# A streaming batch-norm kernel: one input piece loaded over another queue, and the store of the second half in two parts

## The chip, the cores and the metric

The kernel runs on one core of a Trainium2 chip. The metric is the device time of one execution in microseconds, lower being better. The median of three runs of the kernel before is 83.81 us, between 83.76 and 83.91. The profile shows one execution on the same core, with the bytes moved by its 16 DMA engines, the instructions of its compute engines, and the DMA issues of its two issuing queues: SP (the sync engine) and ACT (the scalar engine, which also computes).

## The reference

Inference-time batch normalization followed by a ReLU, in float32, on x of shape 32 x 128 x 32 x 32 (16.78 MB in, 16.78 MB out). Each of the 128 channels has its own mean, variance, gamma and beta:

```
normalized = (x - running_mean[c]) / sqrt(running_var[c] + eps)
out        = maximum(normalized * gamma[c] + beta[c], 0)
```

The work for one element is a multiplication, an addition and a maximum: out = relu(scale[c] * x + bias[c]) with scale = gamma / sqrt(var + eps) and bias = beta - mean * scale.

## The kernel before, in words

The 4096 rows of x (batch times channel, 1024 floats or 4 KB each) are cut into two halves t = 0 and t = 1 of 8.39 MB. In one half, partition p of the on-chip memory holds the 16 neighbouring rows p*16 to p*16+15, so one half is 128 partitions by 16 rows, a run of 64 KB per partition in DRAM. Row number j within a partition fixes the channel together with p, so each j has one column of scale and bias, one value per partition.

All of x fits on the chip, and every piece has its own buffer that is never reused. `TILES` names the pieces as (t, first j, last j): in the first half rows 0-2, 2-4, 4-8 and 8-16, in the second half one tile of all 16 rows. `LOAD_CUTS` cuts the load of that last tile in two at row 8. So there are six loads, all issued by the SP queue (line 54), in this order: 1, 1, 2, 4, 4 and 4 MB, with runs of 8, 8, 16, 32, 32 and 32 KB. A load is 128 such runs, eight on each of the 16 DMA engines.

The four parameter vectors (512 bytes each) are loaded by the ACT queue (line 61) into `raw`, 8 partitions of 16 values. PE spreads them to 128 partitions with a matmul against a 0/1 matrix `rep` built on POOL (line 76), ACT takes the square root (line 84), and DVE makes `scale_t` and `bias_t` in four short instructions (lines 86 to 92).

Then comes the loop on ACT: 32 activations in place, one per (t, j), each 128 x 1024 (line 98). After the last row of a tile, ACT itself issues the store of it (line 106); `STORE_CUTS` adds a store after the very first row. So there are six stores: rows 0, 1, 2-4, 4-8 and 8-16 of the first half (0.5, 0.5, 1, 2 and 4 MB, with runs of 4, 4, 8, 16 and 32 KB), and one store of 8 MB with runs of 64 KB for the whole second half, after its sixteenth activation.

The order on ACT is the written one (the loop stands in a manual schedule), and the order on SP is that of the loads. The framework adds the semaphore waits. It has eight DMA semaphores and hands them out in turn, so a DMA that gets a semaphore which an earlier DMA had must wait for that earlier one to land: on SP, the fourth, fifth and sixth load wait for a parameter load, another parameter load and the second load; on ACT, the last store waits for the first store. The DMA traffic of SP is queue q1 in the profile, that of ACT is q10; both are served by the same 16 DMA engines.

Of the kernel before, what the change touches and what calls it, by code (L numbers as in the profile page):

```python
# [1 line left out]

# [4 lines left out]


F32 = mybir.dt.float32
ACTF = mybir.ActivationFunctionType  # L10

J = 16

TILES = ((0, 0, 2), (0, 2, 4), (0, 4, 8), (0, 8, 16), (1, 0, 16))

LOAD_CUTS = {(1, 8)}
STORE_CUTS = {(0, 1)}


@with_exitstack
def kernel(
    ctx: ExitStack,
    tc: tile.TileContext,
    x: bass.AP,
    gamma: bass.AP,
    beta: bass.AP,
    running_mean: bass.AP,
    running_var: bass.AP,  # L30
    eps: bass.AP,
    out: bass.AP,
):
    nc = tc.nc
    B, C, H, W = x.shape
    HW = H * W
    P = nc.NUM_PARTITIONS
    assert C % J == 0 and P % (C // J) == 0 and (B * C) % (P * J) == 0
    Q = C // J
    T = B * C // (P * J)  # L40

    xr = x.rearrange("b c h w -> (b c) (h w)").rearrange("(t p j) w -> t p j w", p=P, j=J)
    outr = out.rearrange("b c h w -> (b c) (h w)").rearrange("(t p j) w -> t p j w", p=P, j=J)

    data = ctx.enter_context(tc.tile_pool(name="data", bufs=1))
    params = ctx.enter_context(tc.tile_pool(name="params", bufs=1))
    psum = ctx.enter_context(tc.tile_pool(name="psum", bufs=1, space=bass.MemoryType.PSUM))

    tiles = []
    for t, a, b in TILES:  # L50
        xt = data.tile([P, b - a, HW], F32, name=f"x{t}_{a}")
        cuts = [a] + [j for j in range(a + 1, b) if (t, j) in LOAD_CUTS] + [b]
        for c, d in zip(cuts, cuts[1:]):
            nc.sync.dma_start(out=xt[:, c - a : d - a, :], in_=xr[t, :, c:d, :])  # L54
        tiles.append((t, a, b, xt))

    raw = params.tile([Q, 4, J], F32, name="raw")
    for k, src in enumerate((running_var, gamma, running_mean, beta)):  # L60
        nc.scalar.dma_start(out=raw[:, k, :], in_=src.rearrange("(q j) -> q j", j=J))
    eps_t = params.tile([P, 1], F32, name="eps_t")
    nc.vector.memset(eps_t, float(eps))  # L63
    rep = params.tile([Q, P // Q, Q], F32, name="rep")
    nc.gpsimd.memset(rep, 1.0)  # L65
    nc.gpsimd.affine_select(  # L66
        out=rep,
        in_=rep,
        compare_op=mybir.AluOpType.is_equal,
        fill=0.0,  # L70
        base=0,
        pattern=[[0, P // Q], [-1, Q]],
        channel_multiplier=1,
    )
    cols = psum.tile([P, 4, J], F32, name="cols")
    nc.tensor.matmul(  # L76
        cols.rearrange("p k j -> p (k j)"),
        rep.rearrange("q r s -> q (r s)"),
        raw.rearrange("q k j -> q (k j)"),
        start=True,  # L80
        stop=True,
    )
    std_t = params.tile([P, J], F32, name="std_t")
    nc.scalar.activation(out=std_t, in_=cols[:, 0, :], func=ACTF.Sqrt, bias=eps_t[:, 0:1], scale=1.0)  # L84
    rstd_t = params.tile([P, J], F32, name="rstd_t")
    nc.vector.reciprocal(out=rstd_t, in_=std_t)  # L86
    scale_t = params.tile([P, J], F32, name="scale_t")
    nc.vector.tensor_mul(out=scale_t, in0=cols[:, 1, :], in1=rstd_t)  # L88
    ms_t = params.tile([P, J], F32, name="ms_t")
    nc.vector.tensor_mul(out=ms_t, in0=cols[:, 2, :], in1=scale_t)  # L90
    bias_t = params.tile([P, J], F32, name="bias_t")
    nc.vector.tensor_sub(out=bias_t, in0=cols[:, 3, :], in1=ms_t)  # L92

    with tc.manual_schedule(engines={mybir.EngineType.Activation}):
        for t, a, b, xt in tiles:
            first = a
            for j in range(a, b):
                nc.scalar.activation(  # L98
                    out=xt[:, j - a, :],
                    in_=xt[:, j - a, :],  # L100
                    func=ACTF.Relu,
                    bias=bias_t[:, j : j + 1],
                    scale=scale_t[:, j : j + 1],
                )
                if j + 1 == b or (t, j + 1) in STORE_CUTS:
                    nc.scalar.dma_start(
                        out=outr[t, :, first : j + 1, :], in_=xt[:, first - a : j + 1 - a, :]
                    )
                    first = j + 1


# [1 line left out]
_INS = ['x', 'gamma', 'beta', 'running_mean', 'running_var', 'eps']  # L113
_OUTS = [((32, 128, 32, 32), 'float32')]

_NUMBERS = {'eps': 1e-05}


# [26 lines left out]
```

## Time and profile before

| what | value |
|---|---|
| median of the runs | 83.81 us (83.76 to 83.91) |
| the profiled execution's own time | 83.91 us |
| its span in the profile | 81.9 us |
| bytes read and written | 16.78 MB and 16.78 MB |
| mean rate over the span | 410 GB/s |
| ACT busy | 38.5 us, 47% of the span |
| share of 16 DMA engines taken by q1 (loads) and q10 (stores, parameters) | 48.7% and 47.7% |
| first activation of x starts | 9.49 us |
| last activation ends, its store is issued | 56.05 us, 56.08 us |

The span runs from the first to the last instruction of the profiled execution; 2.0 us of its time lie outside. The DMA rows count each DMA packet, which is one run of bytes of a transfer (4 to 64 KB here) or a completion mark of 4 bytes. A packet is booked as a whole at its start, so short windows with long packets show shares above 1 and of 0 beside each other; only their mean over several packets means anything.

### The profile page before, as it was taken

Reading aid. Unit: us, or ns where it says so; the run is one execution under the profiler, and the core shown is the slowest. Engines: PE = TensorE matmul, PEld = TensorE weight load, DVE = VectorE, ACT = ScalarE, POOL = GpSimd, SP = SyncE. Lnnn points to the kernel's source line nnn. Section 1 sums busy time; section 2 is a strip of 40 time slices with the busy share of each in tenths; the row PEclk is TensorE's granted clock in tenths of the full one; section 3 lists DMA queues with packets and bytes.
Section 4 is the critical chain, followed back from the end, with each engine's and each line's share of the span. In section 5 each row is a group of like instructions: output and inputs, shape, how many; then the busy total and the mean of one; then the engine's idle time right before and its main releaser. Section 6 shows DMA issues by size and latency. Waiting matters only on the chain.

```text
span 81.9 us, 118 instructions
## 1 busy us (share of the span) xinstructions
PE 0.7 (1%) x2; PEld 0.5 (1%) x2; DVE 0.8 (1%) x5; ACT 38.5 (47%) x34; POOL 0.8 (1%) x6
## 2 busy tenths in 40 slices
PE   0003000000000000000000000000000000000000
PEld 0002000000000000000000000000000000000000
DVE  0000300000000000000000000000000000000000
ACT  0600477799039999189995099993000000000000
POOL 3000000000000000000000000000000000000000
DMA  3799998989999997969889699997992899998290
GB/s 56 316 437 465 392 560 336 528 336 476 388 400 464 390 474 324 572 296 568 352 368 592 272 464 416 512 448 320 512 769 128 384 512 512 512 512 384 128 512 0
DMA packets 1792, 33.56 MB, mean 410 GB/s; under 512 B 256, under 2 KB 256, under 8 KB 512
## 3 DMA queue, kind: packets, MB, share of 16 engines
q1 hardware_dynamic: 864, 16.78, 48.7%
q10 hardware_dynamic: 928, 16.78, 47.7%
HBM read 16.78 MB, written 16.78 MB: 410 GB/s over the span
## 4 chain that ended last, share of the span: by engine, by line
DMA 56%; ACT 10%; issue 2%; SPq 0%
DMA x<-in_x_dram 56%; ACT x L98 10%; SPq L54 0%
## 5 line engine op out<-in xcount | busy, mean ns | idle before, releaser
L98 ACT ACTIVATE x<-x,bias_t,scale_t 128x1024 f32<-128x1024 f32 x32 | 37.0, 1227 | 10.6 <-DMA x<-in_x_dram 8.3
L84 ACT ACT_TABLE_LOAD x1 | 1.3, 1283 | 2.6 <-issue 2.6
L84 ACT ACTIVATE std_t<-cols,eps_t 128x16 f32<-128x16 f32 x1 | 0.3, 273 | 4.4 <-PE cols L76 4.4
L76 PE MATMUL cols<-raw,rep 8*128 8x64 f32 x2 | 0.7, 429 | 7.5 <-DMA raw<-in_beta_dram 7.5
L76 PEld LDWEIGHTS cols<-raw,rep 8*128 8x128 f32 x2 | 0.5, 306 | 7.5 <-issue 7.5
L66 POOL TENSOR_SCALAR_AFFINE_SELECT rep<-rep 8x128 f32<-8x128 f32 x1 | 0.4, 393 | 0.1
L86 DVE RECIPROCAL rstd_t<-std_t 128x16 f32<-128x16 f32 x1 | 0.3, 253 | 7.6 <-ACT std_t L84 7.6
L65 POOL MEMSET rep<- 8x128 f32 x1 | 0.2, 195 | 0.3 <-POOLq L126 0.3
L88 DVE TENSOR_TENSOR scale_t<-cols,rstd_t 128x16 f32<-128x16 f32 x1 | 0.2, 175 | 0.1
L92 DVE TENSOR_TENSOR bias_t<-cols,ms_t 128x16 f32<-128x16 f32 x1 | 0.2, 175 | 0.0
L90 DVE TENSOR_TENSOR ms_t<-cols,scale_t 128x16 f32<-128x16 f32 x1 | 0.2, 175 | 0.0
L126 POOL MEMSET const-bfloat16-1.0<- 128x1 bf16 x1 | 0.1, 106 | 0.0
L126 POOL MEMSET const-uint8-127<- 128x1 uint8 x1 | 0.1, 106 | 0.0
L126 POOL MEMSET const-float32-0.0<- 128x1 f32 x1 | 0.1, 103 | 0.3 <-issue 0.3
L126 POOL MEMSET const-float32-1.0<- 128x1 f32 x1 | 0.1, 103 | 0.0
L63 DVE MEMSET eps_t<- 128x1 f32 x1 | 0.1, 59 | 0.9 <-PEq L126 0.9
## 6 DMA issues: line engine op xcount, KB each, us to landing
x<-in_x_dram SPq DMA_DIRECT2D x3, 4096.0 KB, 38.7
out_dram<-x ACTq DMA_DIRECT2D x1, 4096.0 KB, 28.6
x<-in_x_dram SPq DMA_DIRECT2D x2, 1024.0 KB, 5.8
x<-in_x_dram SPq DMA_DIRECT2D x1, 2048.0 KB, 11.3
out_dram<-x ACTq DMA_DIRECT2D x1, 2048.0 KB
out_dram<-x ACTq DMA_DIRECT2D x2, 512.0 KB, 19.1
out_dram<-x ACTq DMA_DIRECT2D x1, 1024.0 KB
raw<-in_running_var_dram ACTq DMA_DIRECT2D x1, 0.5 KB
```

What stands on the lines that cost most here:

```text
L63: nc.vector.memset(eps_t, float(eps))
L65: nc.gpsimd.memset(rep, 1.0)
L66: nc.gpsimd.affine_select(out=rep, in_=rep, compare_op=mybir.AluOpType.is_equal, fill=0.0, base=0, pattern=[[0, P // Q], [-1, Q]], channel ...
L76: nc.tensor.matmul(cols.rearrange("p k j -> p (k j)"), rep.rearrange("q r s -> q (r s)"), raw.rearrange("q k j -> q (k j)"), start=True, s ...
L84: nc.scalar.activation(out=std_t, in_=cols[:, 0, :], func=ACTF.Sqrt, bias=eps_t[:, 0:1], scale=1.0)
L86: nc.vector.reciprocal(out=rstd_t, in_=std_t)
L88: nc.vector.tensor_mul(out=scale_t, in0=cols[:, 1, :], in1=rstd_t)
L90: nc.vector.tensor_mul(out=ms_t, in0=cols[:, 2, :], in1=scale_t)
L92: nc.vector.tensor_sub(out=bias_t, in0=cols[:, 3, :], in1=ms_t)
L98: nc.scalar.activation(out=xt[:, j - a, :], in_=xt[:, j - a, :], func=ACTF.Relu, bias=bias_t[:, j : j + 1], scale=scale_t[:, j : j + 1],)
L126: nc = _bacc.Bacc("TRN2", target_bir_lowering=False, num_devices=1)
```

## The change

`TILES` and `LOAD_CUTS` become one table `PIECES` in which load and tile are the same thing, so the second half is now two tiles of eight rows. Their loads are the two 4 MB loads with 32 KB runs that there were. Because a store follows the end of each tile, the single store of 8 MB with runs of 64 KB becomes two of 4 MB with runs of 32 KB, the first of them issued after the eighth activation of the second half. `PIECES_SCALAR` names the piece (0, 2), rows 2-4 of the first half, whose 1 MB load is now issued on the ACT queue, where it stands in front of the four parameter loads. SP issues the other five.

```diff
-TILES = ((0, 0, 2), (0, 2, 4), (0, 4, 8), (0, 8, 16), (1, 0, 16))
+PIECES = (((0, 2), (2, 4), (4, 8), (8, 16)), ((0, 8), (8, 16)))
 
-LOAD_CUTS = {(1, 8)}
 STORE_CUTS = {(0, 1)}
+
+PIECES_SCALAR = (0, 2)
...
-    for t, a, b in TILES:
-        xt = data.tile([P, b - a, HW], F32, name=f"x{t}_{a}")
-        cuts = [a] + [j for j in range(a + 1, b) if (t, j) in LOAD_CUTS] + [b]
-        for c, d in zip(cuts, cuts[1:]):
-            nc.sync.dma_start(out=xt[:, c - a : d - a, :], in_=xr[t, :, c:d, :])
-        tiles.append((t, a, b, xt))
+    for t in range(T):
+        for a, b in PIECES[t]:
+            xt = data.tile([P, b - a, HW], F32, name=f"x{t}_{a}")
+
+            eng = nc.scalar if (t, a) == PIECES_SCALAR else nc.sync
+            eng.dma_start(out=xt, in_=xr[t, :, a:b, :])
+            tiles.append((t, a, b, xt))
```

The semaphores are handed out anew. The fourth load on SP (rows 0-8 of the second half) now waits for the 2 MB load of rows 4-8, and the fifth (rows 8-16 of the second half) for a parameter load. The first store on ACT waits for the 1 MB load that moved, and the new last store for the first store.

## The prediction

> **What bounds the kernel now.** I read the busy shares first, then the DMA queues, the windows, and at last ACT's timeline and the chain. On the page, the busy row of ACT, the DMA row of the slices, the two queues and the chain:
>
> ```profile
> PE 0.7 (1%) x2; PEld 0.5 (1%) x2; DVE 0.8 (1%) x5; ACT 38.5 (47%) x34; POOL 0.8 (1%) x6
> ...
> DMA  3799998989999997969889699997992899998290
> ...
> q1 hardware_dynamic: 864, 16.78, 48.7%
> q10 hardware_dynamic: 928, 16.78, 47.7%
> ...
> DMA 56%; ACT 10%; issue 2%; SPq 0%
> ```
>
> No compute engine is busy half of the time, while the two queues together take 96.4% of the DMA engines' span. Lower digits in the DMA row stand beside packets as long as a slice (booked whole where they start), so they don't yet prove gaps. The windows settle that; columns are window and length, the busy time of PE, PEld, DVE, ACT and POOL, the clock, the DMA share and GB/s:
>
> ```profile
> 1.80:80.70 78.90, 0.66 (x2) 0.50 (x2) 0.78 (x4) 38.51 (x34) 0.00 (x0) 1.00 1.00 425
> 51.70:61.10 9.40, 0.00 (x0) 0.00 (x0) 0.00 (x0) 4.35 (x4) 0.00 (x0) 1.00 1.03 446
> 61.70:78.60 16.90, 0.00 (x0) 0.00 (x0) 0.00 (x0) 0.00 (x0) 0.00 (x0) 1.00 1.00 434
> ```
>
> From 1.80 us (first bytes, 1.0 us after the first issue) to 80.70 us the share is 1.00: all 16 DMA engines always have a packet. The time is therefore the first byte at 1.8, plus 78.9 us of packets, plus 1.2 us of closing down to the span's end, plus 2.0 us outside the span. Whatever happens on ACT, SP or PE counts only if it empties the DMA queues. The chain (its DMA share is 56%) follows ACT's last wait on a load back and does not go through the stores that end last, so I don't read the bound from it. ACT's timeline shows how far the stores are from running dry:
>
> ```profile
> 9.49 1.24 ACT L98 ACTIVATE x<-x,bias_t,scale_t 128x1024 f32<-128x1024 f32 x1 [1.03 <-DVE bias_t L92]
> ...
> 33.13 0.34 ACTq L106 DMA_DIRECT2D out_dram<-x  x1
> 35.01 9.16 ACT L98 ACTIVATE x<-x,bias_t,scale_t 128x1024 f32<-128x1024 f32 x8 [1.91 <-DMA x<-in_x_dram]
> 46.89 9.16 ACT L98 ACTIVATE x<-x,bias_t,scale_t 128x1024 f32<-128x1024 f32 x8 [2.73 <-DMA x<-in_x_dram]
> 56.08 0.34 ACTq L106 DMA_DIRECT2D out_dram<-x  x1
> ```
>
> The loads have landed by 46.89. The 8 MB store is issued at 56.08, and by the trace's packet records its first packet runs at 61.0, right behind the last one of the 4 MB store in front. It is thus some 4 us early (61.0 less 56.08, less about 1 us from issue to first byte). That is a thin margin, but it isn't used up.
>
> **The change part by part.**
>
> 1. *One 8 MB store becomes two of 4 MB.* The packet records give 2.418 us for each 64 KB packet and 1.213 us for a 32 KB packet of a store. Each engine had 8 of the first and now has 16 of the second: 19.344 becomes 19.408 us, +0.064 us, wholly on the path since the engines are never idle. One more DMA adds one completion mark per engine, 9 ns, and a change of transfers: in the records the packets of one store follow the mark of the store before within 6 ns. That is +0.015 us, sum +0.08 us. Bounds for the extra transfer: 0 from below (its work can't be negative) and from above ACT's issue of a store, 0.37 us, if the engines stood still for it. I take 0.015, because it was measured at just such a change from store to store.
> The first half of this store is now issued when the eighth activation ends (35.01 + 9.16 = 44.2) and not at 56.08. That would only gain something if the queue were empty between, and the window to 80.70 says it isn't. The last store now needs 16 packets, 9.70 us, for itself, so it has until about 80.7 - 9.7 - 1.0 = 70.0 us to be issued; it comes at about 56.1 as before. The margin grows from 4 to 14 us, worth nothing here. ACT's one more issue costs 0.34 us plus about 0.4 us of gap, and comes in front of a 2.73 us wait for the last load: hidden.
>
> 2. *The 1 MB load of rows 2-4 goes to ACT's queue.* Its eight packets per engine stay as long as they were. SP loses one issue of about 0.4 us, and its next loads are issued that much earlier; behind the first load, 2.5 us of packets per engine cover this, so nothing is gained. The new waits on SP: its fourth load waits for the rows 4-8 to land (12.1 to 12.6 us before; similar after, since the same 4 MB lie in front) and its fifth for a parameter load (7 to 13 us, next step). Each has the 4 MB load of rows 8-16 in front of it, which lands after 23 us: hidden.
> At the start both queues now issue a 128-run transfer at 0.81 us. Before, SP's x load and the small parameter load went together; SP's issue took 0.37 us, ACT's 0.59 against 0.29 to 0.38 for its later ones. First bytes came at 1.75 (parameter) and at 1.80 to 2.11 on 15 engines, 2.3 on the last. From below: without the parameter in front 0.05 us can go, and if the second queue fills the engines that start late, the ramp of 0.3 us. From above: if the two transfers are written out in turn, the ramp doubles, +0.3 us on the last engines. I take 0: the nearest row is the start of before, which had both queues issuing at once as well.
>
> 3. *The parameters come later.* Their four issues move back by one issue, 0.4 to 0.6 us, and stand behind 1 MB on ACT's queue. In the records the two queues alternate packet by packet once both have work (parameter packets 0.31 us apart beside 8 KB packets). So rows 0-2 and 2-4 share the engines until about 1.8 + 16 x 0.309 + 0.5 (slow first packets) = 7.2 us, and the eight small packets of an engine (four runs, four marks) then alternate with 16 KB packets of 0.611 us: 4.9 us, landing at about 12.1 against 7.46 before. If they are not held up, 7.5. PE, the square root, DVE's four instructions and all activations move with it: the first activation starts at 9.5 to 14.2 instead of 9.49. This is 4.7 us at most, and ACT has waits of 3.65 + 1.91 + 2.73 = 8.3 us for x later on: absorbed before the last load. Even without that: 32 activations of 1.145 us (9.16 over 8) and six issues with gaps of some 0.45 us are 39 us, so ACT could start as late as 70.0 - 39 = 31 us. In between only loads run, at a full share, as they did before the first store. Cost 0.
>
> Sum: 83.91 (this execution) + 0.08 + 0 + 0 = 83.99; this execution lies 0.10 above the median of the runs, so 83.89 against 83.81. I forecast 83.9.
>
> A rule against the change: the Trainium skill, "DMA: Bandwidth & Descriptors", section "Rules for kernel authors", advises coalescing transfers, and its section "Anatomy of one DMA" fits a fixed cost of about 2.0 us per transfer on the GpSimd path. If that stood on the path here, one more store would make 85.9. The 6 ns between two queued stores in this trace speak against it: the fixed part is latency, and the queue hides it.
>
> **The rivals.**
>
> *Slower by the start.* Place: the first issues at 0.81. Two transfers of 128 runs written out together make the last engines begin 0.3 us later; everything behind is saturated, so it appears one to one: 83.9 + 0.3 = 84.2. ACT's first issue of 0.59 us speaks for it, the 2.5 us of packets behind each first packet against it. It decides from 0.1 us of delay (0.17 less the 0.08).
>
> *Slower by the parameters*: decided when ACT starts later than 31 us; at 35 us the end would be 4 us later, 87.9. My latest estimate is 14.2.
>
> *Faster by the start.* The second queue feeds engines that wait in the ramp, and the first packets (0.5 to 1.1 us instead of 0.309 in the records) overlap: up to 0.3 us less, 83.6. Against it: an engine that runs a packet is counted as busy, and two packets at once are rare in the records.
>
> *Other disturbance of the loads.* 67 of 384 load packets of 32 KB took 1.23 to 1.42 us, together 0.36 us per engine, mostly in clusters between 12 and 32 us, where most have stores beside them. Stores that start up to 5 us later meet other loads: between 0 and twice that, so 83.5 to 84.3.
>
> *The change does nothing at all*: 83.81, within the likeliest.
>
> **How the numbers follow.** About 0.2% (0.17 us) is what can be told from no change. Within it 0.50 (the sum, or nothing). Slower 0.32: by the start 0.22, by disturbed loads 0.06, by a dead time at the extra transfer or the parameters 0.04. Faster 0.18: by the start 0.10, fewer disturbed loads 0.08. The likeliest alone has 83.65 to 83.98; the range takes in both starts and both ends of the disturbed loads: 83.5 to 84.3.
>
> **What the next profile would show.** Right: a DMA share of 1.00 from about 1.8 to 80.8; 32 KB packets of 1.213 us to the end; a store issued near 44.2; first activation at 9.5 to 14.5; the last store issued near 56. Wrong: the first bytes or the last engine's start moved by over 0.1 us, a window with a share below 1 between the loads' end and the last byte, a last store issued after 70, or a sum of packet times that differs from 78.9 + 0.08 by over 0.15 us.

## The result, and the profile after

The changed kernel is slower: 84.56 us (84.40 to 84.68) against 83.89 us (83.76 to 84.03) for the kernel before in the same runs, a ratio of 1.0079 with a 95% interval of 1.0064 to 1.0094, or +0.67 us. The prediction had no change, 83.9, with a range of 83.5 to 84.3; 84.56 lies above it.

The page of the changed kernel, the same rows as before:

```profile
PE 0.7 (1%) x2; PEld 0.5 (1%) x2; DVE 0.8 (1%) x5; ACT 38.5 (47%) x34; POOL 0.8 (1%) x6
...
DMA  1899897996999897979799999988996997999690
...
q10 hardware_dynamic: 1216, 17.83, 50.4%
q1 hardware_dynamic: 720, 15.73, 45.8%
...
DMA 54%; ACT 10%; issue 2%; SPq 1%
```

Bytes, engine work and the share of the DMA engines (96.2%) are as they were; the span is 82.7 us and not 81.9. The timeline:

```profile
13.00 0.66 PE L78 MATMUL cols<-raw,rep 8*128 8x64 f32 x2 [13.00 <-DMA raw<-in_beta_dram]
...
15.00 1.24 ACT L100 ACTIVATE x<-x,bias_t,scale_t 128x1024 f32<-128x1024 f32 x1 [1.02 <-DVE bias_t L94]
16.27 0.38 ACTq L108 DMA_DIRECT2D out_dram<-x  x1
...
35.79 9.16 ACT L100 ACTIVATE x<-x,bias_t,scale_t 128x1024 f32<-128x1024 f32 x8 [0.42 <-ACT x L100]
44.98 0.34 ACTq L108 DMA_DIRECT2D out_dram<-x  x1
46.16 9.16 ACT L100 ACTIVATE x<-x,bias_t,scale_t 128x1024 f32<-128x1024 f32 x8 [1.21 <-DMA x<-in_x_dram]
55.35 0.34 ACTq L108 DMA_DIRECT2D out_dram<-x  x1
```

Parameters, first activation and first store come 5.5 us later, 0.8 us more than in the prediction's long case; ACT catches up, and its last store is even issued 0.7 us earlier than before. So nothing starved. The windows show the loss. Of the changed kernel, in the columns explained above:

```profile
1.80:81.40 79.60, 0.66 (x2) 0.50 (x2) 0.78 (x4) 38.51 (x34) 0.00 (x0) 1.00 1.00 422
...
20.90:36.00 15.10, 0.00 (x0) 0.00 (x0) 0.00 (x0) 13.99 (x13) 0.00 (x0) 1.00 1.01 433
41.30:45.70 4.40, 0.00 (x0) 0.00 (x0) 0.00 (x0) 3.65 (x4) 0.00 (x0) 1.00 0.94 333
```

And the last two of these windows in the kernel before:

```profile
20.90:36.00 15.10, 0.00 (x0) 0.00 (x0) 0.00 (x0) 10.15 (x9) 0.00 (x0) 1.00 1.01 430
...
41.30:45.70 4.40, 0.00 (x0) 0.00 (x0) 0.00 (x0) 2.86 (x3) 0.00 (x0) 1.00 1.03 443
```

Divide GB/s by the share, and you have what busy engines move. From 20.9 to 36.0 that is 429 after and 426 before. From 41.3 to 45.7, where the loads end, it is 443 / 1.03 = 430 before and 333 / 0.94 = 354 after. The engines are busy, but their packets take longer. The packet records say which: load packets of 32 KB take 1.213 us at best, and what they take beyond that adds up to 0.36 us per engine before and 1.02 after, of which 0.73 is in the last two packets of the last load (16 packets of 1.76 us on average, then 16 of 1.40). That +0.66 us, with +0.07 for the split store and -0.15 in the first 8 KB packets, makes the sum of packet times 79.48 us per engine against 78.90 (+0.58), and the last completion mark comes at 81.40 against 80.68 (+0.71 before rounding).

### The profile page after: what moved, and what is told of

Its sections match the earlier page's. It is cut to its first block, busy times and chain, and to the rows that moved or that the text cites. A ratio compares the mean times of both kernels' runs of the same rounds, so it can differ in the third digit from the quotient of the medians.

```text
span 82.7 us, 121 instructions
## 1 busy us (share of the span) xinstructions
PE 0.7 (1%) x2; PEld 0.5 (1%) x2; DVE 0.8 (1%) x5; ACT 38.5 (47%) x34; POOL 0.8 (1%) x6
## 4 chain that ended last, share of the span: by engine, by line
DMA 54%; ACT 10%; issue 2%; SPq 1%
DMA x<-in_x_dram 54%; ACT x L100 10%; SPq L56 1%
```

## The experiments

All times are medians beside the kernel before in the same runs, which stood between 83.81 and 83.84. "Slow time" is what the 32 KB load packets of the profiled execution took beyond 1.213 us each, per DMA engine (the sum over all, divided by 16); its parts are those of the first, second and third 4 MB load. Before it is 0.28 + 0.07 + 0.01, in the changed kernel 0.27 + 0.02 + 0.73. It is read from one profiled execution of each kernel, which need not have the median time; where the two differ by more than 0.1 us, the time of that execution is given too.

### Which part of the change

**Only the split store** (the moved load goes back to SP):

```diff
-PIECES_SCALAR = (0, 2)
+PIECES_SCALAR = None
```

> The second half is stored in two parts of 4 MB, the load of rows 2-4 stays on SP. Late stores (the theory: the moved load pushes parameters and first stores back by 5.5 us, and the 32 KB loads are slowed): first activation at 9.5, excess of the 32 KB load packets about 0.36 us per engine as before, 83.95 to 84.05. Cost of the split (rival): 84.4 to 84.6. Start with two queues (rival): 83.9 to 84.0.

83.84 us, ratio 0.9994 (0.9984 to 1.0003); slow time 0.21 + 0.06 + 0.02. The split costs nothing that can be measured.

**Only the moved load** (on the kernel before):

```diff
-            nc.sync.dma_start(out=xt[:, c - a : d - a, :], in_=xr[t, :, c:d, :])
+            eng = nc.scalar if (t, c) == (0, 2) else nc.sync
+            eng.dma_start(out=xt[:, c - a : d - a, :], in_=xr[t, :, c:d, :])
```

> The load of rows 2-4 goes to the ACT queue in front of the parameters, the second half is stored as one 8 MB transfer. Late stores: first activation near 15.0, slow 32 KB loads again, 84.4 to 84.5. Cost of the split: 83.9. Start with two queues: 84.0 to 84.1, with the 32 KB loads no slower than before.

84.23 us, 1.0043 (1.0028 to 1.0058); slow time 0.25 + 0.03 + 0.62. The loss comes with the moved load, but less of it than the 84.4 to 84.5 expected: 0.40 us of 0.67, though the split alone costs nothing. In the trace the first activation waits for the parameters as in the changed kernel, and the last completion mark comes almost as late (81.29 against 81.40); of the profiled executions' own times (84.17 and 84.59), 1.7 and 1.9 us lie outside the span. Why the two times differ by more than the packets do isn't shown.

**Parameters in front of the moved load** (the changed kernel, the four `raw` loads written ahead of the loads of x):

> The changed kernel, but the four parameter loads stand in front of the load of rows 2-4 on the ACT queue. Late stores: parameters land by about 7, first activation before 10, 32 KB loads as before, 83.9 to 84.1. Cost of the split, and start with two queues: as the changed kernel, 84.4 to 84.6.

84.53 us, 1.0074 (1.0060 to 1.0087); slow time 0.22 + 0.01 + 0.67. The expected cure failed. It was a half measure, though: the parameters landed at 9.26, the first store was issued at 12.52 and not 10.76, and rows 2-4, now behind them, landed so late that the third store was issued at 22.55 against 15.27 before. So this run doesn't yet tell late stores from the other queue.

**Late parameters without the moved load** (the kernel before, with the parameter loads issued on SP behind the load of rows 4-8):

```diff
         tiles.append((t, a, b, xt))
+        if (t, a) == (0, 4):
+            raw = params.tile([Q, 4, J], F32, name="raw")
+            for k, src in enumerate((running_var, gamma, running_mean, beta)):
+                nc.sync.dma_start(out=raw[:, k, :], in_=src.rearrange("(q j) -> q j", j=J))
```

> The kernel before with one edit: the four parameter loads are issued on SP behind the load of rows 4-8 and so land at about 12.5. Nothing else moves, the 8 MB store stays. Late stores: first activation near 14.5, slow 32 KB loads, 84.3 to 84.6. Cost of the split, and start with two queues: 83.9, no change.

84.33 us, 1.0057 (1.0037 to 1.0077); slow time 0.22 + 0.05 + 0.80 in a profiled execution that itself took 84.91. The loss is there with all loads of x on SP and a single 8 MB store. But the last loads were issued late here too, at 13.07 and 13.55, as in the changed kernel (13.10 and 13.47) and not at 6.74 and 8.12. The next two runs part these.

**Late issue of the last loads alone**, and **late stores alone**, both on the kernel before. For the first, a DVE copy of a column of rows 4-8 into the tile of the second half makes its loads wait; for the second, eps is computed from a column of rows 4-8, so the activations wait:

```diff
+        if t == 1:
+            for c in cuts[:-1]:
+                nc.vector.tensor_copy(out=xt[:, c - a, 0:1], in_=tiles[2][3][:, 0, 0:1])
...
-    nc.vector.memset(eps_t, float(eps))
+    nc.vector.tensor_scalar(
+        out=eps_t, in0=tiles[2][3][:, 0, 0:1], scalar1=0.0, scalar2=float(eps),
+        op0=mybir.AluOpType.mult, op1=mybir.AluOpType.add,
+    )
```

> The kernel before, but the two loads of the second half are issued on SP only when the load of rows 4-8 has landed (near 13, as in the four slower kernels; a DVE copy of one column into their tile makes them wait). Activations and stores stay as early as before. Theory that the start of the stores decides: 83.8 to 83.95, 32 KB loads slowed by about 0.36 us per engine. Rival, that the late issue of the last loads decides: 84.2 to 84.5, with 0.6 to 0.8 us of slowing in the last load.

> The kernel before, but eps_t is made by DVE from a column of the rows 4-8 (times zero, plus eps), so the square root, all activations and all stores wait for that load, while the issue of all loads and of the parameters stays early. First activation near 14.5. Theory that the start of the stores decides: 84.2 to 84.5, slow packets in the last load. Rival, late issue of the loads: 83.8 to 83.95.

Late issue: 83.70 us, 0.9981 (0.9970 to 0.9991), slow time 0.21 + 0.02 + 0.01; the loads were issued at 13.28 and 13.70. It costs nothing, and this is the fastest kernel of all, by a hair. Late stores: 84.72 us, 1.0103 (1.0080 to 1.0125), slow time 0.20 + 0.06 + 0.84; that is even more than the 84.2 to 84.5 expected. First the window at the end of the loads with the late issue, then the late start on ACT and the windows with late stores:

```profile
41.40:45.60 4.20, 0.00 (x0) 0.00 (x0) 0.00 (x0) 2.68 (x3) 0.00 (x0) 1.00 1.04 449
```

```profile
15.86 1.24 ACT L101 ACTIVATE x<-x,bias_t,scale_t 128x1024 f32<-128x1024 f32 x1 [1.02 <-DVE bias_t L95]
17.13 0.38 ACTq L109 DMA_DIRECT2D out_dram<-x  x1
```

```profile
36.00:41.40 5.40, 0.00 (x0) 0.00 (x0) 0.00 (x0) 4.98 (x6) 0.00 (x0) 1.00 1.02 437
41.40:45.60 4.20, 0.00 (x0) 0.00 (x0) 0.00 (x0) 4.20 (x4) 0.00 (x0) 1.00 0.99 338
```

With the late issue busy engines move 449 / 1.04 = 432 GB/s there. With late stores it is 428 up to 41.4, then 341. All loads and parameters were issued as early as before; only the activations, and with them the stores, began some 6 us later. That alone brings the whole loss and 0.2 us more.

### Where the slow packets belong

**Stores behind all loads**, on one queue (the kernel before, `nc.scalar` becomes `nc.sync` in the store), and the same with the activations waiting for the last load:

```diff
-                    nc.scalar.dma_start(
+                    nc.sync.dma_start(
...
-    nc.vector.memset(eps_t, float(eps))
+    nc.vector.tensor_scalar(
+        out=eps_t, in0=tiles[4][3][:, 8, 0:1], scalar1=0.0, scalar2=float(eps),
+        op0=mybir.AluOpType.mult, op1=mybir.AluOpType.add,
+    )
```

> The kernel before, but the stores are issued on SP and so stand behind all loads in the same queue: reads first, then writes. If the slow load packets come from writes that run among the reads: no slow 32 KB packets, loads end near 41, time 83.4 to 83.6. If the reads are slow by themselves at certain addresses: slow packets at the end of the loads all the same, 83.9 to 84.4. If the queue runs dry between loads and stores: above 84.5, with DMA windows below a share of 1 near 41.

> Stores on SP behind all loads, and eps_t is made from the last load, so no activation and no store exists until all of x has landed. Near 105 us as a whole; what counts are the packets of the last load. Theory A, the last packets of the last load are slow by themselves (addresses, or the end of the loads): its 7th and 8th packets on each engine take 1.4 to 2.2 us again. Theory B, the slowing comes from a store that stands next in the queue: all 32 KB packets 1.21 us, loads end at 41.5.

Stores behind the loads: 84.64 us, 1.0088 (1.0069 to 1.0108), slow time 0.00 + 0.00 + 1.12. The expected gain didn't come: the loads run clean until their last two packets per engine, and those take 1.84 and 1.69 us. With no store in existence until 46 us (104.52 us as a whole, a single run), the slow time is 0.02 in all, and no load packet takes over 1.221 us. The same window, at the end of the loads, first with stores waiting in the queue, then without any:

```profile
38.80:42.40 3.60, 0.00 (x0) 0.00 (x0) 0.00 (x0) 2.86 (x3) 0.00 (x0) 1.00 0.95 286
```

```profile
38.80:42.40 3.60, 0.00 (x0) 0.00 (x0) 0.15 (x1) 0.05 (x1) 0.00 (x0) 1.00 0.64 273
```

Here the loads alone end inside the window, so the share is 0.64, but what busy engines move is 273 / 0.64 = 427 GB/s against 286 / 0.95 = 301 with stores next in line. By the records the first store packet began at 42.36, when all the slow load packets were under way (the last began at 41.41). Nor did the queue run dry: first byte at 1.735 plus 79.696 us of packets is 81.43, and the last marks come at 81.43 on average. ACT's work is no rival either: it is idle in the second kernel, but in the first it was busy for 6.30 of the 6.80 us from 32.0 to 38.8, with no load packet over 1.25 us. So the reads are slowed when stores follow them, and not by their own addresses; by what mechanism, no record shows.

**Another order of the loads.** Once with stores behind the loads, rows 8-16 of the first half last; once the changed kernel with the two parts of the second half exchanged:

```diff
-TILES = ((0, 0, 2), (0, 2, 4), (0, 4, 8), (0, 8, 16), (1, 0, 16))
+TILES = ((0, 0, 2), (0, 2, 4), (0, 4, 8), (1, 0, 16), (0, 8, 16))
...
-PIECES = (((0, 2), (2, 4), (4, 8), (8, 16)), ((0, 8), (8, 16)))
+PIECES = (((0, 2), (2, 4), (4, 8), (8, 16)), ((8, 16), (0, 8)))
```

> Stores on SP behind all loads, but the second half is loaded (and processed) ahead of rows 8-16 of the first half, which come last. If the slow packets belong to addresses: the 7th and 8th packets of rows 8-16 of the second half are slow, now in the middle of the loads, and the last load is clean. If they belong to the place where stores take over from loads: the last two packets of the load of rows 8-16 of the first half are slow.

> The changed kernel with the two parts of the second half in the other order (rows 8-16 first, rows 0-8 last; loads, activations and stores). If the slow packets belong to addresses: 7th and 8th packets of rows 8-16 of the second half slow although that load is now the last but one. If they belong to the end of the loads: those of rows 0-8 of the second half slow, 84.3 to 84.7 as the changed kernel. If neither, 83.9 to 84.1.

84.68 us (a single run) with slow time 0.01 + 0.00 + 1.20, and 84.54 us, 1.0077 (1.0056 to 1.0099), with 0.24 + 0.00 + 0.62. The slow packets stay with whichever load is last. They belong to the place where stores take over.

### Why the hand-over is free in the kernel before

**Three theories**: the place within the store that runs beside the end (P), the size of the packets beside it until then (S), the late start by itself (T). The edits are cuts of the first stores, in the changed kernel and twice in the kernel before:

```diff
-STORE_CUTS = {(0, 1)}
+STORE_CUTS = set()
...
-STORE_CUTS = {(0, 1)}
+STORE_CUTS = {(0, 1), (0, 3)}
...
-STORE_CUTS = {(0, 1)}
+STORE_CUTS = set()
```

> The changed kernel without the cut of the first store: rows 0-2 leave as one store of 1 MB with 8 KB runs, so the first store starts even later (about 21), the queue of stores carries 8 KB packets to the end of the loads, and the store of rows 2-4 is then at its last packets. Theory P (the hand-over from loads to stores is dear when the store beside the last load packets is at its first packets, and free when it is at its last): no slow packets at the end, 83.9 to 84.1. Theory S (dear when 4 KB packets were beside the loads until then): 83.9 to 84.1. Theory T (dear whenever the stores start late): 84.3 to 84.7.

> The kernel before with rows 2-4 also stored in two parts, four stores of 4 KB runs in all: stores start early, and the packets beside the end of the loads are 4 KB ones, of a store that is at its last packets. P and T: 83.8 to 84.0. S: 84.2 to 84.7.

> The kernel before without the cut of the first store: early stores of 8 KB runs, so that the store beside the last load packets is that of rows 4-8 (16 KB runs), about in its middle. P: partly dear, 84.0 to 84.4. S and T: 83.7 to 83.9, a little less than before for 128 packets of 8 KB in place of 256 of 4 KB.

The changed kernel without the cut: 84.11 us, 1.0037 (1.0026 to 1.0049), slow time 0.46 + 0.13 + 0.00. The end is free although the stores start late, so T falls; but the first 8 KB packets, coming beside the 7th and 8th packet of the first load, now cost more (0.46). The kernel before with a second cut: 84.52 us, 1.0074 (1.0056 to 1.0093), slow time 0.15 + 0.00 + 0.70. Early stores and a dear end: T falls again, and P with it, since this store was at its last packets. The kernel before without the cut: 83.96 us, 1.0012 (0.9998 to 1.0025), slow time 0.45 + 0.13 + 0.19 in a profiled execution that itself took 84.20, with nothing in the last two packets of the last load. S foretold all three ends; the costs at the start it did not.

The end of the loads with 4 KB packets beside it (the kernel before, cut twice), and with 8 KB packets (the changed kernel without a cut):

```profile
41.40:45.60 4.20, 0.00 (x0) 0.00 (x0) 0.00 (x0) 2.51 (x3) 0.00 (x0) 1.00 0.83 287
```

```profile
41.40:45.60 4.20, 0.00 (x0) 0.00 (x0) 0.00 (x0) 3.34 (x3) 0.00 (x0) 1.00 1.00 429
```

That is 346 GB/s for busy engines against 429.

**Is it the size of the packets that come next?** (theory N). The changed kernel with rows 2-8 stored at once in 24 KB runs, and three kernels with stores behind all loads whose first store has runs of 64, 16 or 8 KB. Two parts of these edits are left out below (`...`): the loop of the changed kernel cuts a load at `LOAD_CUTS` as that of the kernel before does, so that the six loads stay as they are, and the stores behind the loads are issued with `nc.sync`.

```diff
-PIECES = (((0, 2), (2, 4), (4, 8), (8, 16)), ((0, 8), (8, 16)))
+PIECES = (((0, 2), (2, 8), (8, 16)), ((0, 8), (8, 16)))
+
+LOAD_CUTS = {(0, 4)}
...
-TILES = ((0, 0, 2), (0, 2, 4), (0, 4, 8), (0, 8, 16), (1, 0, 16))
+TILES = ((0, 0, 16), (1, 0, 16))
 
-LOAD_CUTS = {(1, 8)}
-STORE_CUTS = {(0, 1)}
+LOAD_CUTS = {(0, 2), (0, 4), (0, 8), (1, 8)}
+STORE_CUTS = set()
...
```

(16 KB: `{(0, 4), (0, 8)}`; 8 KB: `{(0, 2), (0, 4), (0, 8)}` as the store cuts.)

> The changed kernel with one edit: rows 2-4 and 4-8 of the first half leave as one store with 24 KB runs, in place of one with 8 KB and one with 16 KB. The start stays as late, the queue at the end of the loads now holds 24 KB packets. Theory N (what counts is whether packets of 8 KB or less stand next in the store queue when the loads end): 83.9 to 84.1, no slow packets in the last load. Theory L (the late start by itself): 84.4 to 84.6.

> Stores on SP behind all loads, the first half as one tile and one store of 8 MB with 64 KB runs (loads of it as before, in four pieces). N: no slow packet at all, loads end at 41.4, then 38.7 us of stores without a gap, 83.2 to 83.5, faster than the kernel before. If any hand-over of all engines at once costs: 84.0 to 84.5, with the last two load packets of each engine slow.

> As sp_64k, but the first half is stored in parts of 4, 4 and 8 rows, so 16 packets of 16 KB per engine come first after the loads. N with a limit between 8 and 16 KB: no or little slowing, 83.3 to 83.7. A cost that grows as packets get smaller: 0.1 to 0.6 us of slowing in the last two load packets.

> As sp_64k, but the first half is stored in parts of 2, 2, 4 and 8 rows, so 16 packets of 8 KB per engine come first after the loads. N: last two load packets of each engine slow by 0.6 to 1.1 us together, 84.0 to 84.6. If packet size is not the cause: as sp_64k.

The changed kernel with 24 KB runs: 84.24 us, 1.0048 (1.0033 to 1.0063), slow time 0.12 + 0.00 + 0.42 in a profiled execution of 84.11; less, but not gone. Behind the loads: 84.82 us, 1.0120 (1.0103 to 1.0137) with 64 KB, a single run each of 84.59 with 16 KB and 84.50 with 8 KB, and a slow time of 1.14, 1.14 and 1.05, all in the third load. N falls: a hand-over from loads with nothing beside them costs 1.05 to 1.20 us of slow time whatever comes next. And the kernel with 64 KB, which N had as faster than the kernel before, is the slowest of these.

**S in the changed kernel itself**: only row 0 leaves in 4 KB runs, rows 1-4 follow as one store of 12 KB runs.

```diff
-PIECES = (((0, 2), (2, 4), (4, 8), (8, 16)), ((0, 8), (8, 16)))
+PIECES = (((0, 4), (4, 8), (8, 16)), ((0, 8), (8, 16)))
+
+LOAD_CUTS = {(0, 2)}
...
```

> The changed kernel with another cut of the first stores: row 0 alone (4 KB runs), then rows 1-4 as one store with 12 KB runs, in place of two 4 KB stores and one of 8 KB. The second queue, the late parameters and the split store stay. Theory S (the hand-over is dear when until then nothing or only 4 KB packets ran beside the loads, and free when packets of 8 KB or more did): the 4 KB packets end near 31, 12 KB packets run beside the whole last load, no slow packets there, 83.8 to 84.0. Theory L (late start by itself): 84.3 to 84.6, with 0.6 to 0.8 us of slowing in the last two load packets.

84.29 us, 1.0051 (1.0038 to 1.0065). The last load is clean (0.00), as S has it, but the time didn't come back: slow time 0.05 + 0.58 + 0.00. The loss has moved to where the 4 KB packets give way to 12 KB ones, at the 7th packet of the second load. Three windows of this kernel, before, at and behind that step:

```profile
20.90:30.60 9.70, 0.00 (x0) 0.00 (x0) 0.00 (x0) 9.28 (x9) 0.00 (x0) 1.00 1.05 441
30.60:34.90 4.30, 0.00 (x0) 0.00 (x0) 0.00 (x0) 4.30 (x4) 0.00 (x0) 1.00 0.97 378
34.90:44.40 9.50, 0.00 (x0) 0.00 (x0) 0.00 (x0) 9.08 (x9) 0.00 (x0) 1.00 0.99 426
```

Busy engines move 420, then 390, then 430 GB/s.

Put together, each step up in what is stored beside the loads, with the slow time of the load it falls in:

| store packets beside the loads, from -> to | where | slow time, us per engine |
|---|---|---|
| none -> stores alone (any run, 4 to 64 KB) | end of the loads | 1.05 to 1.20 |
| none -> 8 KB | first load | 0.45, 0.46 |
| none -> 4 KB | first load | 0.05 to 0.28 |
| 4 KB -> stores alone | end of the loads | 0.70 |
| 4 KB -> 8 KB, then stores alone | last two packets of the last load | 0.62 to 0.84 |
| the same, the 8 KB three packets earlier on eight engines (parameters in front) | last two packets of the last load | 0.67 |
| 4 KB -> 12 or 24 KB | 7th packet of a load | 0.58, 0.42 |
| 8 KB -> 8 KB (next store; the changed kernel without the cut) | 8th packet of the second load | 0.13 |
| 8 KB -> 16 KB | 3rd to 5th packet of the last load | 0.19 |
| 8, 12 or 16 KB -> 16 KB or stores alone | end of the loads | 0.00 to 0.02 |
| 4 KB -> 8 KB | behind the 1st packet of the last load (kernel before, only the split store, late issue) | 0.01, 0.02 |

Shown: late stores by themselves bring the loss; loads with no store about are clean (0.02 us); and most of the slow time stands where something more comes to be stored beside the loads, most of all where nothing was stored before. Not shown is that the size of the step sets the price: 4 to 24 KB cost 0.42 us, 4 to 12 KB 0.58. Nor is a step always needed: 0.07 us of the kernel before stand at the 7th packet of the second load, in the middle of a store of 4 KB packets.

The run with the parameters in front also speaks against S in its plain form. By its packet records the 8 KB packets began on eight of the 16 engines at 39.2 to 39.5 us, and the 24 load packets behind them took 1.213 us but for one of 1.228; still, the last load packet of each of these engines took 1.39 to 2.07. So the step from 4 to 8 KB cost nothing there, and three 8 KB packets beside the loads didn't free the end. Whether three are too few, or what happens on the other engines counts, isn't shown.

Why the last row is free isn't shown either, nor what in the DMA engines or the memory makes the loss. Place and lateness go together here: a store and a load of 128 packets each take the same number of turns, so once stores run, each change of store falls at the same place in its load. In the changed kernel the marks between stores come at about 30.7 and 41.6 us, between the 6th and 7th load packet; in the kernel before at about 24.6 and 35.6, between the 1st and 2nd. No run moved that place alone on all engines. This stays open.

## Why the prediction was wrong, point by point

- *What bounds the kernel* was read half right. The engines do have a packet all the time, before and after. Wrong was the sentence that whatever happens on ACT, SP or PE counts only if it empties the DMA queues. A share of 1.00 says that a packet is in work, not that it moves at full speed: 430 GB/s and 354 GB/s both stand under a share near 1. Late stores cost 0.88 us (84.72 against 83.84) with no queue empty.
- *Step 1, the split store*: right. 16 packets of 1.213 us per engine, +0.07 us by the records, and 0.9994 by itself. The fixed cost of about 2.0 us per transfer, which the Trainium skill gives in "DMA: Bandwidth & Descriptors", section "Anatomy of one DMA", for the GpSimd path, doesn't appear on this queue.
- *Step 2, the moved load*: its parts held. The first bytes came at 1.80 us against 1.75, and the engines were through the first two loads at 7.42 us on average against 7.38, so the start was worth 0.04 us and neither start rival came true. The late issue on SP is free, as the run with the late issue alone shows.
- *Step 3, the parameters*: **this is the step that failed.** Its delay was nearly right (matmul at 13.0 where 12.1 was the late end, first activation at 15.0 where 14.2 was), and ACT absorbed it as said. "Cost 0" was the error: the cover was taken to be loads at full share, and what the later stores do to the pace of the loads was left out. The term put at 0 measured 0.88 us by itself (late stores), and 0.73 us of slow packets stand at the end of the loads in the changed kernel. Because the 4 KB stores begin 5 us later, they stay beside the loads until 40.6 us, where before 8 KB packets had been there since 36.7.
- *The rival of disturbed loads* named the right packets, but with 0 to 0.72 us of slow time and no sign. It was 1.02, and it wasn't chance: every kernel whose 4 KB stores reached the last packets of the loads had 0.42 to 0.84 us in the last load. The clusters of slow packets in the trace of before were the hint. Most of them stand between 13 and 21 us, where the stores begin (first store packet at 14.5), and at 31.4; the prediction had a number for them but didn't ask what set it. (Its count is off a little: 59 load packets took 1.23 us or more; 67 took 1.223 or more.)

## What to carry to other kernels

When a kernel is bound by its transfers, divide the bytes moved by the busy share, stage by stage; a full share with fewer GB/s is a loss that no idle time shows (430 and 354 GB/s here). A load that is put in front of small ones on a queue delays all that hangs on them (parameters at 13.0 and not 7.5 us), and even if every engine has slack for it, the mix of loads and stores moves. Here the three fastest kernels (the one before, the split store alone, the late issue) began their stores early and had 8 KB packets beside nearly all of the last load; that this is a rule isn't shown. So try such orders on the chip: the edits here were worth between 0.2% less and 1.2% more time, and the expected gain of several of them (parameters in front, stores behind the loads, 64 KB runs, 12 KB runs) didn't come or not in full.

## What the runs showed that was not expected

- Writing behind all reads, on one queue, is not the fast way. It is clean until the turn and then loses 1.05 to 1.20 us of slow time there, with 4 to 64 KB runs alike, and loads slow down before a single store packet has begun.
- The cure for one step brought the cost back at the next: the end of the loads got free with 12 KB runs, and 0.58 us appeared at the 7th packet of the load before.
- Issuing the last two loads 5.6 to 6.5 us later made the kernel, if anything, faster: 83.70 us, 0.9981 (0.9970 to 0.9991).
